# Four more turns behind each triangular solve's copies, a later due time for the last pair's transposes, and the decode queries' fill and rearrangement on other engines

## The chip, the cores and the metric

One NeuronCore of a Trainium2 chip runs the whole program in one launch. The metric is the device time of an execution in microseconds (us); the value for a kernel is the median of its runs.

## The reference

One inference step of a decoder layer: 512 prompt tokens of width 2048 and 8 decode tokens that attend to a cache. A norm, modulated by a conditioning vector (adaLN), is followed by one input projection w_in, whose columns feed two mixers: sliding-window attention (16 query heads, 4 key/value heads) and RWKV-7 (16 heads of 64 channels). Both outputs go through w_out; a SwiGLU FFN follows. Of mixer B this is what the change touches:

```python
def _wkv7_scan(S0, r, w, k, v, a, b):
    def step(S, inp):
        r_t, w_t, k_t, v_t, a_t, b_t = inp
        sa = jnp.einsum("bhij,bhj->bhi", S, a_t)
        S = S * w_t[:, :, None, :] + sa[..., None] * b_t[:, :, None, :] + v_t[..., None] * k_t[:, :, None, :]
        return S, jnp.einsum("bhij,bhj->bhi", S, r_t)
...
# mixer B, per head: y from the scan, then group norm over the 64 channels, bonus, gate
    y, S = _wkv7_scan(S0.astype(f32), r_h, hs(decay), k_h, v_h, -kk, kk * hs(a))
    mu = jnp.mean(y, axis=-1, keepdims=True)
    var = jnp.mean(jnp.square(y - mu), axis=-1, keepdims=True)
    y = ((y - mu) * lax.rsqrt(var + GN_EPS)).reshape(B, T, RWKV_WIDTH) * ln_w + ln_b
    bonus = jnp.sum(r_h * k_h * r_k.astype(f32), axis=-1, keepdims=True) * v_h
    y = (y + bonus.reshape(B, T, RWKV_WIDTH)) * g
...
# mixer A: sliding-window attention (window 128, ALiBi, sinks); w_out on both mixers' outputs; SwiGLU FFN
```

## The kernel before

All four engines and the DMA queues work on one stream. TensorE (PE) multiplies in three passes (a weight tile split into `wh` and `wl`, activations into `hH` and `hL`), two products of 260 columns each, so one k-step of a w_in or w_out tile is six matmuls. A weight tile is loaded by SP (`raw`), cast on ACT (`wh`) and subtracted on VectorE, DVE in the profile (`wl`), and serves four k-steps, 24 matmuls.

Stages: start (adaLN of this layer, norm), the RWKV part (140 to 920 us) with eight head pairs, attention with w_out beside it (from 915 us), then the FFN. In the RWKV part the w_in tiles (`main_tile`) are the filler, and everything else comes as generators ("jobs"). After each k-step `pump` adds 0.62 us to a planner's clock and resumes each job whose due time has passed; `self.done_at` is the due time that a job leaves behind, and wrapped engines add the estimated cost of what they issue. A bare `yield` hands the turn back until the next k-step. A scheduler then orders each engine's instructions by their dependences and this program order, so a shift of a job can move everything behind it.

The steps of one pair, in its order:

- prep: elementwise work on DVE, ACT and POOL, then products `pG` on PE, masked to `AB` on DVE, and rearranged through DRAM (`ABd`, tile `As`, queues of POOL and SP).
- solve (`rwkv_rest`): the inverse of 32x32 unit triangular blocks, 31 steps of two DVE operations on `Tt` (lines 721 and 724), with other DVE work between them. Its result goes to DRAM in four DMAs on POOL and SP (`TTd`, line 731), comes back in one on POOL (`Td`, line 732), and four DVE copies put it into the block-diagonal `TT`.
- turns: the loop of line 738 gives back the turn. Then two groups of four products `pu` = L3 x `TT` (shown as `pu<-TT,L`).
- chain: 16 steps on PE and ACT through `Z` (psum `psc`), the output products `pY`, the group norm on DVE and ACT (tile `RR`), line 804's due time, and four transposes of the normed `RR` (psum `pt2`, shown as `pt<-cst,RR`). Their result becomes `V`, is gated, written to DRAM (`catd`) and read back (`catl`) as input of w_out.

adaLN of the FFN runs beside the pairs in small products `ada<-ar,cT`, whose loads `ar` SP issues. SP's and POOL's queues are in order: an issue that waits holds all issues behind it.

Decode attention (`attn_decode`): the decode queries `QS` are rearranged by two DMAs into `QW` (lines 980 and 981), a tile `Q4` (in the profile `rstd`, whose buffer it takes) is zeroed (line 983), and eight DVE copies put `QS` and `QW` in it. Prompt attention issues logits `pl`, softmax on DVE (`Lg`, `sm`), transposes `pt<-cst,Lg` and the product `pO`, with w_out matmuls `po` as filler.

Of the kernel before, what the change touches and what calls it, by code (L numbers as in the profile page):

```python
# [63 lines left out]
class Kern:  # L64
# [642 lines left out]
    def rwkv_rest(self, d):  # L707
        nc, I, rc = self.px, self.I, self.rc
        hp, L3, PC = (d[n] for n in ("hp", "L3", "PC"))
# [25 lines left out]
        for c4 in range(4):  # L735
            ro = slice(32 * c4, 32 * c4 + 32)
            nc.vector.tensor_copy(TT[ro, :, 32 * c4:32 * c4 + 32], Td[ro])
        for _ in range(4):
            yield
        for e in range(2):  # L740
            pu = self.aux("pu")
# [59 lines left out]
        nc.scalar.activation(var, var, AF.Sqrt, bias=self.eps_g, scale=1.0 / 64)  # L801
        nc.vector.reciprocal(var, var)
        nc.vector.tensor_tensor(g3(yc), g3(yc), b3(var), ALU.mult)
        self.done_at = self.now() + 1.8
        yield
        pt = self.aux("pt2")
        for q in range(4):
# [164 lines left out]
    def attn_decode(self):  # L972
        nc, I, ap = self.px, self.I, self.ap
# [4 lines left out]
        QW = ap.tile([P, 8, 8], F32, name="QW")  # L978
        QS = self.QS.rearrange("p t h s -> p t (h s)")
        for b in range(2):  # L980
            nc.gpsimd.dma_start(QW[64 * b:64 * b + 64], QS[64 - 64 * b:128 - 64 * b])
        Q4 = xt("rstd")[:, 0:512].rearrange("p (a b c) -> p a b c", a=2, b=8)
        nc.gpsimd.memset(Q4, 0.0)
        yield
        for hg in range(2):
            rows = slice(64 * hg, 64 * hg + 64)
# [768 lines left out]
```

## Time and profile before

| | us |
|---|---|
| median of 3 runs | 2652.13 (2649.76 to 2660.87) |
| profiled execution | 2657.65 |
| its span in the profile | 2655.8 |
| PE busy | 2539.9 (96%) |
| DVE, ACT, POOL busy | 1648.6, 1166.6, 384.7 |
| granted TensorE clock, mean | 0.976 |
| PE idle, 140 to 920 us / 920 to 1050 us | 44.2 / 11.2 |

The span is the profiled execution from its first instruction to its last. A row of the timeline gives start, duration, engine, line, operation, out<-in, shapes, the count of like rows drawn together, and in brackets the engine's idle time before it with what released it. Line L49 is the wrapper through which the jobs issue, so most of the pairs' rows carry it and are told apart by their tiles.

### The profile page before, as it was taken

Reading aid. Unit: us, or ns where it says so; the run is one execution under the profiler, and the core shown is the slowest. Engines: PE = TensorE matmul, PEld = TensorE weight load, DVE = VectorE, ACT = ScalarE, POOL = GpSimd, SP = SyncE. Lnnn points to the kernel's source line nnn. Section 1 sums busy time; section 2 is a strip of 40 time slices with the busy share of each in tenths; the row PEclk is TensorE's granted clock in tenths of the full one; section 3 lists DMA queues with packets and bytes.
Section 4 is the critical chain, followed back from the end, with each engine's and each line's share of the span. In section 5 each row is a group of like instructions: output and inputs, shape, how many; then the busy total and the mean of one; then the engine's idle time right before and its main releaser. Section 6 shows DMA issues by size and latency. Waiting matters only on the chain. (4 is left out here: it accounts for less than half of the span.)

```text
span 2655.8 us, 58969 instructions
## 1 busy us (share of the span) xinstructions
PE 2539.9 (96%) x23373; PEld 2368.0 (89%) x23373; DVE 1648.6 (62%) x3627; ACT 1166.6 (44%) x2413; POOL 384.7 (14%) x532
## 2 busy tenths in 40 slices
PE   7898999899999999998999999999999999999998
PEld 4687878777788988898999999999999999999997
DVE  5465545465566454678877777777777763443456
ACT  3143556456555333457544444444444432222225
POOL 0011112121213110011121122122122000000003
PEclk9998999899999998999999999999999999999999
DMA  9865555455334574345586687687687452333333
GB/s 352 300 203 178 182 179 185 152 180 175 124 121 131 178 227 151 100 160 180 167 225 194 173 232 202 165 229 205 165 227 211 124 180 92 124 124 102 118 102 111
DMA packets 241701, 460.20 MB, mean 173 GB/s; under 512 B 32352, under 2 KB 44560, under 8 KB 241392
## 3 DMA queue, kind: packets, MB, share of 16 engines
q1 hardware_dynamic: 206160, 377.22, 43.1%
q0 software_dynamic: 34624, 78.16, 13.4%
q8 instruction: 183, 3.00, 0.5%
q10 hardware_dynamic: 640, 1.05, 0.2%
q14 instruction: 94, 0.77, 0.1%
HBM read 421.73 MB, written 35.59 MB: 172 GB/s over the span
## 5 line engine op out<-in xcount | busy, mean ns | idle before, releaser
L89 ACT CAST wh<-raw 128x512 fp32r<-128x512 f32 (+2 forms) x410 | 247.4, 606 | 490.4 <-PE pf L99 285.1
L92 DVE TENSOR_TENSOR wl<-raw,wh 128x512 fp32r<-128x512 f32 (+2 forms) x410 | 280.0, 686 | 246.8 <-ACT wh L89 230.8
L99 PE MATMUL pf<-go,wh 128*128 128x260 f32 x2560 | 414.1, 281 | 0.0
L99 PEld LDWEIGHTS pf<-go,wh 128*128 128x128 f32 x2560 | 354.0, 188 | 0.1
L1283 ACT CAST wh<-sr 128x512 fp32r<-128x512 f32 x320 | 198.0, 621 | 258.3 <-PE pm L1454 228.5
L99 PE MATMUL pm<-hH,wh 128*128 128x260 f32 (+1 forms) x1248 | 292.4, 312 | 7.6 <-ACT wh L89 6.8
L1284 DVE TENSOR_TENSOR wl<-sr,wh 128x512 fp32r<-128x512 f32 x320 | 220.3, 689 | 83.1 <-ACT wh L1283 76.0
L99 PE MATMUL pf<-go,wl 128*128 128x260 f32 x1280 | 267.7, 282 | 0.0
L99 PE MATMUL pm<-hH,wl 128*128 128x260 f32 (+1 forms) x1248 | 263.4, 290 | 4.2 <-DVE wl L92 4.2
L1454 PE MATMUL pm<-xT,wh 128*128 128x260 f32 x1408 | 263.2, 286 | 1.4 <-DVE pc L1531 1.1
L99 PE MATMUL pm<-hL,wh 128*128 128x260 f32 (+1 forms) x1248 | 260.4, 289 | 0.0
L1454 PE MATMUL pm<-T,wh 128*128 128x260 f32 x1408 | 257.7, 283 | 0.0
L99 PEld LDWEIGHTS pm<-hH,wh 128*128 128x128 f32 (+1 forms) x1248 | 195.9, 190 | 45.5 <-issue 18.7
L1454 PEld LDWEIGHTS pm<-xT,wh 128*128 128x128 f32 x1408 | 216.8, 188 | 7.9 <-DVE pc L1531 3.1
L1454 PEld LDWEIGHTS pm<-T,wh 128*128 128x128 f32 x1408 | 216.9, 188 | 0.0
L1454 PE MATMUL pm<-B0H,wl 128*128 128x260 f32 x704 | 200.8, 285 | 9.4 <-DVE wl L1284 9.0
L99 PEld LDWEIGHTS pm<-hH,wl 128*128 128x128 f32 (+1 forms) x1248 | 196.1, 190 | 13.8 <-DVE wl L92 7.1
L1454 PE MATMUL pm<-B0H,wh 128*128 128x260 f32 x704 | 200.4, 285 | 2.5 <-DVE acct L1220 1.7
L99 PEld LDWEIGHTS pf<-go,wl 128*128 128x128 f32 x1280 | 201.0, 188 | 0.0
L99 PEld LDWEIGHTS pm<-hL,wh 128*128 128x128 f32 (+1 forms) x1248 | 196.4, 191 | 4.7 <-issue 2.5
L1454 PE MATMUL pm<-T,wl 128*128 128x260 f32 x704 | 198.9, 282 | 0.1
L1454 PE MATMUL pm<-B0L,wh 128*128 128x260 f32 x704 | 198.9, 282 | 0.0
(426 smaller groups left out, 5266.8 us busy)
## 6 DMA issues: line engine op xcount, KB each, us to landing
ar<-in_w_ada SPq DMA_DIRECT2D x256, 256.0 KB, 4.0
sr<-in_w_fi SPq DMA_DIRECT2D x176, 256.0 KB, 4.3
raw<-in_w_fo SPq DMA_DIRECT2D x176, 256.0 KB, 2.7
raw<-in_w_in SPq DMA_DIRECT2D x144, 256.0 KB, 3.8
araw<-in_w_ada SPq DMA_DIRECT2D x64, 512.0 KB, 6.6
raw<-in_w_fi SPq DMA_DIRECT2D x120, 256.0 KB, 4.1
s<-in_w_fi SPq DMA_DIRECT2D x80, 256.0 KB, 5.5
s<-in_w_fi POOLq DMA_DIRECT2D x80, 256.0 KB, 7.2
```

Source lines behind the costliest of these rows:

```text
L89: nc.scalar.copy(wh[:, :n], raw[:, :n])
L92: nc.vector.tensor_tensor(wl[:, :n], raw[:, :n], wh[:, :n].bitcast(F32), ALU.subtract)
L99: nc.tensor.matmul(ps[:m, bank, :HB], w, a[:, k, h, :], start=first and i == 0, stop=last and i == 2, skip_group_check=True,)
L1283: nc.scalar.copy(H, src)
L1284: nc.vector.tensor_tensor(L, src, H.bitcast(F32), ALU.subtract)
L1454: nc.tensor.matmul(ps[:, :HB], x[:, s], y, start=g == k == i == 0, stop=g == 1 and k == 3 and i == 2, skip_group_check=True)
```

## The change

Three edits: eight bare yields for four between the copies into `TT` and the products `pu` (all pairs); for the last pair (hp 7) a due time 4.3 us instead of 1.8 behind the group norm; and in the decode part the two `QW` DMAs issued by SP instead of POOL, and the fill of `Q4` on DVE instead of POOL.

```diff
--- before.py
+++ after.py
@@ -735,7 +735,7 @@
         for c4 in range(4):
             ro = slice(32 * c4, 32 * c4 + 32)
             nc.vector.tensor_copy(TT[ro, :, 32 * c4:32 * c4 + 32], Td[ro])
-        for _ in range(4):
+        for _ in range(8):
             yield
         for e in range(2):
             pu = self.aux("pu")
@@ -801,7 +801,7 @@
         nc.scalar.activation(var, var, AF.Sqrt, bias=self.eps_g, scale=1.0 / 64)
         nc.vector.reciprocal(var, var)
         nc.vector.tensor_tensor(g3(yc), g3(yc), b3(var), ALU.mult)
-        self.done_at = self.now() + 1.8
+        self.done_at = self.now() + (1.8 if hp < 7 else 4.3)
         yield
         pt = self.aux("pt2")
         for q in range(4):
@@ -978,9 +978,9 @@
         QW = ap.tile([P, 8, 8], F32, name="QW")
         QS = self.QS.rearrange("p t h s -> p t (h s)")
         for b in range(2):
-            nc.gpsimd.dma_start(QW[64 * b:64 * b + 64], QS[64 - 64 * b:128 - 64 * b])
+            nc.sync.dma_start(QW[64 * b:64 * b + 64], QS[64 - 64 * b:128 - 64 * b])
         Q4 = xt("rstd")[:, 0:512].rearrange("p (a b c) -> p a b c", a=2, b=8)
-        nc.gpsimd.memset(Q4, 0.0)
+        nc.vector.memset(Q4, 0.0)
         yield
         for hg in range(2):
             rows = slice(64 * hg, 64 * hg + 64)
```

What it does to the order of instructions in the RWKV part. The table counts, for each pair, what PE has between the pair's last `pG` and its first `pu`, and how many DVE instructions that are not the solve's stand between its first step and its last, before -> after:

| pair | w_in matmuls | ada products | other DVE instructions in the solve |
|---|---|---|---|
| 1 | 181 -> 186 | 96 -> 85 | 15 -> 15 |
| 2 | 203 -> 197 | 96 -> 80 | 20 -> 17 |
| 3 | 191 -> 204 | 96 -> 103 | 15 -> 15 |
| 4 | 227 -> 174 | 80 -> 80 | 25 -> 6 |
| 5 | 179 -> 186 | 80 -> 96 | 15 -> 8 |
| 6 | 175 -> 184 | 112 -> 80 | 11 -> 10 |
| 7 | 187 -> 250 | 80 -> 64 | 9 -> 8 |
| 8 | 227 -> 230 | 0 -> 0 | 20 -> 28 |

Pair 4's solve on DVE shows it closest. Its last steps before (`stmp` and `Tt` are the solve; `tF`, `KB` are the next pair's preparation, `wl` and `lf` weight tiles):

```order
L724 TENSOR_TENSOR Tt<-Tt,stmp_5922 128x7x4
L49 SCALAR_TENSOR_TENSOR tA_5840<-tF_5740,tA_5840 128x512
L721 TENSOR_TENSOR stmp_5931<-Tt,As 128x24
L92 TENSOR_TENSOR wl_6275<-raw_6272,wh_6274 128x512
L724 TENSOR_TENSOR Tt<-Tt,stmp_5931 128x8x3
L49 TENSOR_TENSOR tF_5740<-tF_5740,tD_5842 128x512
L721 TENSOR_TENSOR stmp_5934<-Tt,As 128x16
L92 TENSOR_TENSOR lf_6332<-raw_6333,lf_6332 128x256
L724 TENSOR_TENSOR Tt<-Tt,stmp_5934 128x8x2
L49 TENSOR_TENSOR KB_6294<-tF_5740,tC_5996 128x16x32
L721 TENSOR_TENSOR stmp_5953<-Tt,As 128x8
L724 TENSOR_TENSOR Tt<-Tt,stmp_5953 128x8
```

And its last steps in the changed kernel:

```order
L721 TENSOR_TENSOR stmp_5966<-Tt,As 128x28
L724 TENSOR_TENSOR Tt<-Tt,stmp_5966 128x7x4
L721 TENSOR_TENSOR stmp_5975<-Tt,As 128x24
L724 TENSOR_TENSOR Tt<-Tt,stmp_5975 128x8x3
L721 TENSOR_TENSOR stmp_5978<-Tt,As 128x16
L724 TENSOR_TENSOR Tt<-Tt,stmp_5978 128x8x2
L721 TENSOR_TENSOR stmp_5997<-Tt,As 128x8
L724 TENSOR_TENSOR Tt<-Tt,stmp_5997 128x8
L49 TENSOR_SCALAR tA_6048<-tA_6048 128x512
```

The next pair's elementwise work no longer stands between the steps.

The last pair's transposes on PE (`pt_...<-cst,RR`; `pm` are w_in tiles, the numbers name the weight tiles) before:

```order
L99 MATMUL pm_11122<-hL,wh_11169 128x260 x2
L99 MATMUL pm_11122<-hH,wl_11170 128x260 x2
L99 MATMUL pm_11122<-hH,wh_11169 128x260 x2
L99 MATMUL pm_11122<-hL,wh_11169 128x260 x2
L99 MATMUL pm_11122<-hH,wl_11170 128x260 x2
L99 MATMUL pm_11122<-hH,wh_11199 128x260
L49 MATMUL pt_1552_11141<-cst,RR_9622 128x128 x4
L99 MATMUL pm_11122<-hH,wh_11199 128x260
L99 MATMUL pm_11122<-hL,wh_11199 128x260 x2
```

and in the changed kernel:

```order
L99 MATMUL pm_11252<-hH,wh_11285 128x260 x2
L99 MATMUL pm_11252<-hL,wh_11285 128x260 x2
L99 MATMUL pm_11252<-hH,wl_11286 128x260 x2
L99 MATMUL pm_11252<-hH,wh_11285 128x260 x2
L99 MATMUL pm_11252<-hL,wh_11285 128x260 x2
L99 MATMUL pm_11252<-hH,wl_11286 128x260
L49 MATMUL pt_1571_11301<-cst,RR_9655 128x128 x4
L99 MATMUL pm_11252<-hH,wl_11286 128x260
L99 MATMUL pm_11252<-hH,wh_11285 128x260 x2
```

Before they stand behind the first matmul of a new weight tile, now behind the seventeenth of the 24 that a tile serves. From the last pair's `pY` to them there were 67 w_in matmuls and are 59; 335 w_in matmuls followed them and 247 follow now.

The first logits of prompt attention on PE (`po_12103` and the next `po` are two output tiles of w_out, 12136 and 12188 weight tiles) before:

```order
L99 MATMUL po_12103<-cH_11273,wh_12136 128x260 x2
L99 MATMUL po_12103<-cL_11274,wh_12136 128x260 x2
L99 MATMUL po_12103<-cH_11273,wl_12137 128x260 x2
L99 MATMUL po_12103<-cH_11273,wh_12136 128x260 x2
L99 MATMUL po_12103<-cL_11274,wh_12136 128x260 x2
L99 MATMUL po_12103<-cH_11273,wl_12137 128x260 x2
L49 MATMUL pl_12158<-Kt,q_12081 128x128
L49 MATMUL pl_12159<-Ks,q_12081 128x128
L49 MATMUL pl_12158<-Kt,q_12081 128x256
```

and in the changed kernel:

```order
L99 MATMUL po_12185<-cH_11398,wh_12188 128x260 x2
L99 MATMUL po_12185<-cL_11399,wh_12188 128x260 x2
L99 MATMUL po_12185<-cH_11398,wl_12189 128x260 x2
L99 MATMUL po_12185<-cH_11398,wh_12188 128x260 x2
L99 MATMUL po_12185<-cL_11399,wh_12188 128x260 x2
L99 MATMUL po_12185<-cH_11398,wl_12189 128x260 x2
L49 MATMUL pl_12212<-Kt,q_12081 128x128
L49 MATMUL pl_12213<-Ks,q_12081 128x128
L49 MATMUL pl_12212<-Kt,q_12081 128x256
```

The logits stood in the last weight tile of `po_12103`; now a further 24 w_out matmuls stand ahead of them. On SP the two `QW` transfers now stand between two loads of w_out tiles, and the fill stands on DVE between two `wl`.

## The prediction

> **What bounds the kernel now.** I read the busy table first, then the waits of TensorE in the two stretches that the change reaches, then the single waits in time order.
>
> ```profile
> PE 2539.9 (96%) x23373; PEld 2368.0 (89%) x23373; DVE 1648.6 (62%) x3627; ACT 1166.6 (44%) x2413; POOL 384.7 (14%) x532
> PEclk9998999899999998999999999999999999999999
> ```
>
> PE is the bound: 116 us of the 2655.8 us span are idle, so only a PE wait, or time at a lower clock, can be won. The next two views are PE's waits from 140 to 920 us (the eight head pairs of the recurrent part) and from 920 to 1050 us (start of attention): what waited <- for what, us in total, times, longest.
>
> ```profile
> PE pu L49 <- DVE TT L49: 17.2, 6, 5.0
> PE psc L49 <- ACT Z L49: 8.8, 13, 1.8
> PE pt L49 <- DVE RR L49: 5.6, 1, 5.6
> ...
> PE pt L49 <- DVE sm L49: 5.9, 1, 5.9
> PE pl L49 <- issue: 4.9, 1, 4.9
> 140.00:920.00 780.00, 735.80 (x8416) 637.71 (x8415) 453.30 (x1105) 400.04 (x987) 144.21 (x197) 0.95 0.51 164
> ```
>
> The last row is a window (start:end, length, busy PE, PEld, DVE, ACT, POOL, then granted clock, DMA share, GB/s): 44.2 us of PE idle in the first stretch, and a clock of 0.95. The 17.2 us stand exactly where edit one puts its turns. PE's rows there, in time order (start, duration, operation, idle before it and its releaser):
>
> ```profile
> 250.27 0.65 PE L322 MATMUL ada<-ar,cT 128*32 128x128 f32 x8 [5.67 <-DMA ar<-in_w_ada]
> 254.46 0.77 PE L49 MATMUL pu<-TT,L 128*128 128x128 f32 x2 [3.02 <-DVE TT L49]
> 328.74 0.38 PE L49 MATMUL pu<-TT,L 128*128 128x128 f32 x1 [1.21 <-DVE TT L49]
> 388.74 0.47 PE L49 MATMUL pu<-TT,L 128*128 128x128 f32 x1 [2.93 <-DVE TT L49]
> 491.86 0.58 PE L49 MATMUL pu<-TT,L 128*128 128x128 f32 x1 [5.05 <-DVE TT L49]
> 562.87 0.58 PE L49 MATMUL pu<-TT,L 128*128 128x128 f32 x1 [1.82 <-DVE TT L49]
> 711.41 0.46 PE L49 MATMUL pu<-TT,L 128*128 128x128 f32 x2 [3.19 <-DVE TT L49]
> ```
>
> These are pairs 1 to 5 and 7; pairs 6 and 8 do not wait. What ends last is the chain behind the solve, here pair 4's on VectorE:
>
> ```profile
> 479.64 0.18 DVE L724 TENSOR_TENSOR Tt<-Tt,stmp 128x8 f32<-128x8 f32 x1
> 490.62 1.18 DVE L49 COPY TT<-Td 32x256 f32<-32x256 f32 x4 [6.52 <-DMA Td<-TTd]
> DMA to landing us min/median/max: 4.0/5.0/6.3
> ```
>
> From the last solve step to the last copy it is 12 us, most of it two DMAs, one behind the other (the last row is the second's time from issue to landing, line 732, over the eight pairs). No edit shortens this chain; more PE work can only be put beside it.
>
> **Edit one, eight turns for four.** One turn is a k-step of six w_in matmuls. Their spacing is:
>
> ```profile
> 951.69 0.40 PE L99 MATMUL po<-cH,wl 128*128 128x260 f32 x2
> 951.93 0.40 PE L99 MATMUL po<-cH,wh 128*128 128x260 f32 x2
> ```
>
> 0.12 us each, so a turn is 0.73 us and four turns 2.9 us, if all four are spent behind the copies. They are not: the order is chosen again, and the table in the section on the change gives the net effect. Per pair, with 0.12 us a w_in matmul and some 0.06 us a small ada product (eight in 0.65 us above):
>
> - Pair 1 gets 5 more w_in matmuls and 11 fewer ada products ahead of pu: nothing. Its 3.02 and 5.67 us are one wait, on the solve: SP issues two of the TTd copies, the loads of `ar` are queued behind them, and an ada product that needs one stands right at pu. I keep 8.7 us.
> - Pair 2: 6 w_in and 16 ada fewer, -1.7 us of cover, against 1.9 us less other VectorE work inside the solve (estimated from the order's shapes). About 1 us of the 1.21 stays.
> - Pair 3: 13 w_in more, 1.6 us, and a few small products. Of 2.93 us some 0.6 stay.
> - Pair 4: 53 w_in fewer, -6.4 us; but the reciprocals and elementwise work between the solve steps go (the first piece of order below the diff), an estimated 11 us. Line 721's steps here span 29.7 us, pair 7's 21.6 (instructions of one line in pair 4's and in pair 7's window; the count, ns min/median/max, first and last start):
>
> ```profile
> L721 DVE TENSOR_TENSOR stmp<-Tt,As x31: 133/249/1222, 449.7 to 479.4; 128x60 f32<-128x60 f32 x3, 128x28 f32<-128x28 f32 x2, 128x54 f32<-128x54 f32 x2, 128x48 f32<-128x48 f32 x2
> ...
> L721 DVE TENSOR_TENSOR stmp<-Tt,As x31: 168/251/1008, 679.7 to 701.3; 128x60 f32<-128x60 f32 x3, 128x28 f32<-128x28 f32 x2, 128x54 f32<-128x54 f32 x2, 128x48 f32<-128x48 f32 x2
> ```
>
>   At pair 7's speed the solve is 8 us shorter, more than the 6.4 lost: of 5.05 us some 0.5 to 3.5 stay, I take 1.
> - Pair 5: 7 w_in and 16 ada more, 1.8 us: gone. Pair 7: 63 w_in more, 7.6 us against 3.19: gone.
>
> Together 1.21+2.93+5.05+1.82+3.19 = 14.2 us, less 2.6 that stay: **-11.6 us**, with bounds of 0 (the waits only move) and -14.2.
>
> Behind the waits the clock was low (windows as above, the clock third from last):
>
> ```profile
> 388.70:392.10 3.40, 3.36 (x15) 2.67 (x15) 0.00 (x0) 1.09 (x2) 0.00 (x0) 0.52 0.20 74
> 491.70:495.10 3.40, 3.24 (x56) 3.02 (x57) 0.80 (x2) 0.59 (x1) 0.20 (x1) 0.50 0.15 39
> 562.70:566.10 3.40, 3.23 (x15) 3.23 (x16) 3.33 (x6) 0.88 (x2) 1.36 (x1) 0.53 0.16 51
> 711.40:714.80 3.40, 3.39 (x24) 2.83 (x25) 0.69 (x1) 1.86 (x4) 0.00 (x0) 1.00 0.00 0
> ```
>
> Three of four 3.4 us windows behind a wait ran at about 0.5, each losing 1.7 us: 5 us if all return. But 3.19 us of wait at 711 cost no clock and 1.82 at 562 did, so the length of the wait alone does not decide, and small products around the same places may keep it low (rival 5). I take **-3.5 us** (bounds 0 and -5.1).
>
> **Edit two, 4.3 for 1.8 in the last pair.**
>
> ```profile
> 876.66 0.69 PE L49 MATMUL pt<-cst,RR 128*128 128x128 f32 x2 [5.56 <-DVE RR L49]
> ```
>
> A later due time would put matmuls ahead of the transposes. The second piece of order shows none: they have moved by eight w_in matmuls within the tiles, to an earlier place if anything: 59 w_in matmuls behind the last pY instead of 67, with the same group norm on VectorE between. **0 us**, bounds -5.6 (wait gone) and +1.0 (8 matmuls less cover). What the wait of 5.56 us costs in clock stays too.
>
> **Edit three, fill and rearrangement off POOL's queue.** The two transfers and the fill themselves, and what waited for them:
>
> ```profile
> 921.46 1.06 POOL L49 DMA_DIRECT2D QW<-QS  x2 [0.38 <-issue]
> 922.51 0.55 POOL L49 MEMSET rstd<- 128x512 f32 x1
> 923.09 0.25 DVE L49 COPY rstd<-QS 64x16 f32<-64x16 f32 x2 [2.22 <-POOL rstd L49]
> ...
> DMA to landing us min/median/max: 5.5/5.6/5.7
> ```
>
> PE's only wait from 920 to 960 us:
>
> ```profile
> PE po L99 <- ACT wh L89: 0.4, 1, 0.4
> ```
>
> So the 2.22 us of VectorE's wait and the 0.55 us of fill, now on VectorE, are worth nothing directly. On SP the two issues (1.06 us on POOL) now stand ahead of loads of w_out; PE's 0.4 us there was all that reached it from such a tile; uncovered the issues cost 1 us. The Trainium skill ("DMA: Bandwidth & Descriptors", Latency and other measured facts) gives about 1 us to the first byte from POOL's queue and 0.6 from SP's: 0.4 us of a 5.6 us transfer, hidden as well.
>
> What it does change is the order after it. PE's two long waits of this stretch:
>
> ```profile
> 948.90 16.14 SPq L49 DMA_DIRECT2D q<-qd  x4
> 960.60 0.55 PE L49 MATMUL pl<-Kt,q 64*128 64x128 f32 x1 [4.91 <-issue]
> DMA to landing us min/median/max: 11.6/12.3/12.9
> ...
> 1013.97 0.62 ACT L144 CAST cH<-catl 128x512 fp32r<-128x512 f32 x1 [6.29 <-DMA catl<-catd]
> 1016.23 0.47 PE L49 MATMUL pt<-cst,Lg 128*128 128x128 f32 x1 [5.89 <-DVE sm L49]
> 1013.50:1020.30 6.80, 4.07 (x16) 3.02 (x17) 3.40 (x14) 1.61 (x3) 0.00 (x0) 0.50 0.48 157
> ```
>
> The first logits waited 4.91 us for the load of `q`, issued at 948.90 and landed some 11.6 us later. In the third piece of order they stand 24 matmuls later, 2.9 us: **-2.9** (bounds 0 and -4.9). At 1016 PE waited for softmax work on VectorE, which stood behind the cast of `catl` on ACT, which waited 6.29 us for its load. In the new order some 78 w_out matmuls (9.4 us) stand between the first pO and the next attention product, and the cast overlaps them: **-4** (bounds 0 and -5.9). The 6.8 us at 0.50 around it lose 3.4 us; I take **-2** (bounds 0 and -3.4).
>
> **The sum.** A new order of 1766 rows on PE will make small waits of its own; the old order has 13 on `Z` of 8.8 us in all, so I allow **+3** (bounds -4 and +9). -11.6 -3.5 +0 -2.9 -4 -2 +3 = **-21 us**. The profiled execution took 2657.65 us (span 2655.8), so 2636.7; the median of the runs, 2652.13, lies 5.5 us under that execution, so I forecast **2631 us**.
>
> **Rivals.**
>
> 1. *The waits only move* (0.26). Where pu no longer waits for TT, PE meets the next late thing: `Z` in the chain behind pu (13 waits already), or the later pt2. For it: the chain solve-to-TT is unchanged, and pair 4's cover shrinks by 6.4 us. Against it: pairs 6 and 8 show that a pair can pass without a wait. Then edit one gives -2, the rest -5: 2645 us; with edit three also empty, 2652.
> 2. *Slower: loads queue behind the solve* (0.08). SP's queue is in order, and its TTd copies wait for the solve:
>
> ```profile
> 243.30 1.33 SPq L731 DMA_DIRECT2D TTd<-Tt  x2
> 245.38 1.81 SPq L317 DMA_DIRECT2D ar<-in_w_ada  x4
> ```
>
>    In pair 1 the `ar` loads behind them cost 5.67 us of PE. More turns ahead of pu use up loaded tiles sooner. If in all seven other pairs an ada product stands ahead of pu whose load is queued behind TTd, each pays 5.7 in place of the 14.2 in all: 7 x 5.7 - 14.2 = +26, less 9 from edit three: 2669 us. It decides from the point where such a load's use is less than about 6 us behind the solve's end. Against it: in the new order only pairs 3 and 5 have one such load ahead of pu, 2 to 3 us before it, which is 9 us behind the solve's end.
> 3. *Edit two does what it says* (0.07): 5.56 us and 1.7 to 3.4 of clock more, 2623 us.
> 4. *Decode costs PE* (0.05): the fill on VectorE (0.55 us) and `QW` on SP delay `wl` and a load; 2 to 4 us at each of two places, and no gain from edit three: 2645 us.
>
> 5. *The clock stays low* (0.12). At 711 a wait of 3.19 us cost no clock and one of 1.82 us at 562 was followed by 3.4 us at 0.53, and the ada products and the pairs' 32- and 64-row products lie around the same places; then the low windows do not come from these waits and stay. The sum loses its terms of 3.5 and 2: 2636.5 us. The Trainium skill ("TensorE: Matmul & The Clock Gate", What's actually happening) has the clock halve after at least one idle window of about 3.4 us, counted on a free-running grid; by that rule the waits of 1.8 to 3.2 us would not do it alone, which is this rival; the windows at 388 and 562, directly behind such waits, speak for the forecast.
>
> **How the numbers follow.** The forecast has 0.42. A measurement of this kernel tells about 0.5% from no change: 13.3 us, so below 2639 or above 2665. Faster by more: most of the forecast (0.38), rival 3 (0.07), most of rival 5 (0.09) and the good end of rival 1 (0.06): 0.60. Slower: most of rival 2, 0.07. The rest is within: 0.33. The range takes the forecast's bounds as far as they are likely to fall together (-38 us: 2614) and, above, rival 1 with its empty end and a little over (2656): **2614 to 2656**.
>
> **What would show it.** Right: PE's waits on TT fall from 17.2 to about 5 us, with pair 1's pair of waits kept; pair 4's solve takes some 21 us; pt waits for RR still 5 to 6 us in the last pair; pl and pt at the start of attention wait 2 us each. Wrong: PE's waits on `ar` or `Z` grow by as much as those on TT fall; the clock of the 140 to 920 stretch stays 0.95; the wait on RR gone.

## The result and the profile after

| | median, us | runs | ratio to before, 95% interval |
|---|---|---|---|
| before | 2651.39 (2648.54 to 2660.87) | 6 | |
| changed | 2633.22 (2630.48 to 2636.15) | 6 | 0.9928 [0.9912, 0.9945] |

The change makes the kernel 18 us faster; 2631 was forecast. The total came out, but not by the terms of the sum. The profiled execution of the changed kernel has a span of 2630.3 us, 25.5 less than the one of before. The medians here and below are those of the fast executions; the one slow execution, 11271 us in e3, is in none of them.

The first two lines of the changed kernel's page:

```profile
PE 2526.8 (96%) x23373; PEld 2359.7 (90%) x23373; DVE 1650.7 (63%) x3628; ACT 1167.3 (44%) x2413; POOL 382.3 (15%) x529
PEclk9998999999999997999999999999999999999999
```

PE's instructions are the same in number, and its busy time fell by 13.1 us: the same matmuls ran faster. Windows over two stages of before and then of the changed kernel show where. The first reaches from 140 us to the first w_out matmul, the second from there to the first FFN product:

```profile
140.00:919.50 779.50, 735.30 (x8412) 637.21 (x8411) 453.30 (x1105) 399.54 (x986) 144.17 (x196) 0.95 0.51 164
919.50:1211.30 291.80, 272.91 (x2301) 250.64 (x2300) 168.45 (x541) 128.55 (x322) 38.47 (x66) 0.95 0.51 161
...
140.00:892.70 752.70, 717.87 (x8461) 627.04 (x8455) 458.12 (x1115) 401.21 (x990) 142.30 (x196) 0.97 0.53 170
892.70:1189.20 296.50, 279.55 (x2301) 254.74 (x2300) 168.72 (x543) 128.98 (x322) 38.00 (x63) 0.94 0.52 160
```

The recurrent part is 26.8 us shorter, the w_out part 4.7 us longer. In the first, PE's idle time (length less busy time) fell from 44.2 to 34.8 us, and the clock rose from 0.95 to 0.97. The trace's clock records give that more closely: the stretches at half clock add up to 71.6 us before and 41.0 after, so with half of each lost, 35.8 and 20.5 us. (PE is idle for 8.2 and 6.2 us of these stretches, and idle time loses nothing by a lower clock; without it the loss is 31.8 and 17.4 us. All figures below count the whole stretches.) Waits gave 9.4 us, the clock 15.3 by this count. The FFN, which the change does not reach, differs by about 3 us between the two profiles.

PE's waits in the recurrent part of the changed kernel, and the single waits for TT and for the last pair's RR:

```profile
PE pu L49 <- DVE TT L49: 18.4, 5, 10.1
PE psc L49 <- ACT Z L49: 6.7, 12, 1.9
PE pt L49 <- DVE RR L49: 4.8, 4, 1.7
...
259.17 0.55 PE L49 MATMUL pu<-TT,L 128*128 128x128 f32 x1 [10.05 <-DVE TT L49]
336.63 0.60 PE L49 MATMUL pu<-TT,L 128*128 128x128 f32 x3 [3.03 <-DVE TT L49]
484.13 0.35 PE L49 MATMUL pu<-TT,L 128*128 128x128 f32 x1 [0.78 <-DVE TT L49]
623.86 0.35 PE L49 MATMUL pu<-TT,L 128*128 128x128 f32 x1 [3.58 <-DVE TT L49]
788.11 0.38 PE L49 MATMUL pu<-TT,L 128*128 128x128 f32 x1 [0.91 <-DVE TT L49]
862.03 0.44 PE L49 MATMUL pt<-cst,RR 128*128 128x128 f32 x2 [1.65 <-DVE RR L49]
```

The sum on TT looks unchanged (17.2, now 18.4), and read alone it would say that the edit failed. But pair 1's two waits, 5.67 on `ar` and 3.02 on TT, are now one of 10.05 on TT. Without pair 1 the waits on TT went from 14.2 us to 8.3, and the wait on `ar` is gone from the list. Pairs 3, 5 and 7 no longer wait; pairs 6 and 8, which did not, now do.

### The profile page after: what moved, and what is told of

Its sections match the earlier page's. It is cut to its first block, busy times and chain, and to the rows that moved or that the text cites. A ratio compares the mean times of both kernels' runs of the same rounds, so it can differ in the third digit from the quotient of the medians.

```text
span 2630.3 us, 58954 instructions
## 1 busy us (share of the span) xinstructions
PE 2526.8 (96%) x23373; PEld 2359.7 (90%) x23373; DVE 1650.7 (63%) x3628; ACT 1167.3 (44%) x2413; POOL 382.3 (15%) x529
```

## The experiments

In every table and text below, "w_in part" is the first window above, its half-clock loss is worked out in the same way, and ratios are to runs of the kernel before on the same chip. A profile is one execution of its kernel and not always a typical one: that of e4 is the slowest of its twelve, 9 us above their median, that of e6 lies 8 us above its median and that of e9 8 us below.

**The edits one by one, and more turns.** e1 holds edit one alone, e2 edit two, e3 edit three; e4 is the changed kernel with twelve turns.

```diff
 e1
-        for _ in range(4):
+        for _ in range(8):
 e2
-        self.done_at = self.now() + 1.8
+        self.done_at = self.now() + (1.8 if hp < 7 else 4.3)
 e3
-            nc.gpsimd.dma_start(QW[64 * b:64 * b + 64], QS[64 - 64 * b:128 - 64 * b])
+            nc.sync.dma_start(QW[64 * b:64 * b + 64], QS[64 - 64 * b:128 - 64 * b])
...
-        nc.gpsimd.memset(Q4, 0.0)
+        nc.vector.memset(Q4, 0.0)
 e4 (against the changed kernel)
-        for _ in range(8):
+        for _ in range(12):
```

> Edit one alone (eight turns for four). Theory 1, from the trace of the changed kernel: the whole gain is in the part up to 920 us and is this edit's, 9 us of PE waits and 15 us of half clock; the ratio to before is 0.988 to 0.993, the end of w_in comes 22 to 28 us earlier, and the last pair's wait for RR is near 1.7 us without edit two. Theory 2, the sizes of the prediction: -12 of waits, -3.5 of clock, a ratio of 0.994 to 0.9955, the wait for RR stays 5 to 6 us.

> Edit two alone (due time 4.3 us in the last pair). In the order of instructions only a few rows of PE, VectorE and ACT change places, and the transposes stay where they were. Theory 1: ratio 0.999 to 1.001, wait for RR 5 to 6 us. Rival: the due time itself ends the wait for RR (1.7 us in the changed kernel), ratio 0.997 to 0.998.

> Edit three alone (QW's transfers on SP, the fill on VectorE). Theory 1, from the trace of the changed kernel: the stretch from the first w_out matmul to the first of the FFN takes 296 us instead of 292, mostly by half clock behind the decode products; ratio 1.000 to 1.003. Theory 2, the prediction: the waits before pl and pt shrink by 9 us together, ratio 0.996 to 0.997.

> The changed kernel with twelve turns instead of eight. If the waits for TT that are left (3.0, 0.8, 3.6 and 0.9 us behind pairs 2, 4, 6 and 8) are a matter of cover, four more turns (2.9 us) end most of them: 3 to 6 us, ratio 0.989 to 0.991. If the gain of eight turns came from where the small products fall among the w_in matmuls, there is no trend: ratio anywhere from 0.988 to 1.000, and the time goes with the sum of half-clock stretches up to the end of w_in (20 us in the changed kernel, 36 before), not with the waits.

| | median, us | ratio, 95% interval |
|---|---|---|
| before | 2656.17 | |
| e1, eight turns alone | 2627.66 | 0.9892 [0.9869, 0.9915] |
| e2, due time alone | 2657.22 | 1.0012 [0.9995, 1.0028] |
| e3, decode alone | 2659.06 | 1.0015 [0.9996, 1.0033] |
| e4, twelve turns | 2645.78 | 0.9955 [0.9934, 0.9975] |

The whole gain is edit one's; neither of the others shows a gain. The last pair's transposes in e2 and e1 decide who ended the wait for RR:

```profile
874.11 0.48 PE L49 MATMUL pt<-cst,RR 128*128 128x128 f32 x1 [5.66 <-DVE RR L49]
...
864.68 0.33 PE L49 MATMUL pt<-cst,RR 128*128 128x128 f32 x1 [1.66 <-DVE RR L49]
```

With the due time alone (first row) the wait stands at 5.66 us; with the turns alone (second row) it is 1.66, as in the changed kernel. How the turns did it is read on VectorE: before and in the changed kernel, the last output products `pY` and the reduction that begins the group norm:

```profile
858.76 1.23 DVE L49 TENSOR_TENSOR stt<-sS,X 128x1024 f32<-128x1024 f32 x1 [5.48 <-DMA sS<-in_st]
861.67 1.17 PE L49 MATMUL pY<-Z,RR 128*32 128x64 f32 x64
869.20 0.68 DVE L49 TENSOR_REDUCE L<-pY 128x8 f32<-128x512 f32 x1
...
851.91 1.17 PE L49 MATMUL pY<-Z,RR 128*32 128x64 f32 x64
855.36 0.68 DVE L49 TENSOR_REDUCE L<-pY 128x8 f32<-128x512 f32 x1
```

Before, the decode state's work (`stt`, `sS`) had waited 5.48 us for a load, stood ahead of the group norm, and the reduction came 7.5 us behind the start of `pY`. Now it comes 3.5 us behind. The same work still stands ahead of it and still waits for its load, 3.70 us, but it starts 7.0 us ahead of `pY` (at 844.91) instead of 2.9.

In e3 the waits for `pl` and `pt` are gone as forecast, and another has come:

```profile
PE plx L49 <- DVE sm L49: 5.5, 1, 5.5
```

The w_out part takes 295.1 us there, against 291.8 and 292.8 in before and e2. PE's idle time in it did fall, to 14.5 us from 18.9 before, but half clock loses 20.3 us of it against 15.4. Where the 5.5 us come from, the changed kernel's timeline shows across four engines:

```profile
926.47 13.64 SPq L49 DMA_DIRECT2D q<-qd  x4
940.21 7.91 SPq L87 DMA_DIRECT2D raw<-in_w_out  x4
946.41 1.23 ACT L89 CAST wh<-raw 128x512 fp32r<-128x512 f32 x2 [11.93 <-DMA raw<-in_w_out]
947.06 0.69 DVE L92 TENSOR_TENSOR wl<-raw,wh 128x512 fp32r<-128x512 f32 x1 [8.60 <-ACT wh L89]
947.67 0.48 DVE L49 CUSTOM_DVE_ANT_0 Lg<-pl,bias,der 128x256 f32<-128x256 f32 x1
948.62 0.21 PE L49 MATMUL plx<-KVS,rstd 64*32 64x1 f32 x1 [5.52 <-DVE sm L49]
```

Four issues of `q` loads hold SP from 926.47 to 940.11, since the last one's buffer is not free; behind them stands a w_out tile's load; the cast waits for it, `wl` for the cast, the softmax work for `wl`, and PE for the softmax. The logits now stand behind that tile's `wl` on VectorE.

e4 speaks against a trend. Its first pair gains what twelve turns promise: PE's waits there (on `ar` and on TT, up to 270 us) are

```profile
PE ada L322 <- DMA ar<-in_w_ada: 3.7, 1, 3.7
PE pu L49 <- DVE TT L49: 1.6, 1, 1.6
```

5.3 us in place of 10.1. But behind it the waits on TT are 15.6 us where eight turns alone have 10.2, and the half-clock loss of the w_in part is 37.5 us against 22.2. The granted clock of all executions, not only of the profiled one, points the same way: 0.9761 on average in e4, 0.9815 in e1, 0.9754 in the kernel before.

**Six turns, and three tries at a better place.** e5 has six turns and nothing else; e6 and e7 are e1 with small products given in smaller portions; e8 is e1 with twelve turns for the first pair.

```diff
 e5 (against before)
-        for _ in range(4):
+        for _ in range(6):
 e6 (against e1), in the loop over c of the pA products
+            if hp < 2 and c in (5, 10):
+                yield
 e7 (against e1), at the end of the decode value products
-            yield
+                yield
 e8 (against e1)
-        for _ in range(8):
+        for _ in range(12 if hp == 0 else 8):
```

> The kernel before with six turns for four, nothing else changed. If the turns work as cover (2 x 0.73 us more beside each chain), the waits for TT behind pairs 2 to 8 lie between those of four turns (14 us) and eight turns (10 us), and the ratio between 0.993 and 0.997. If the gain comes from where the order happens to fall, six turns show no such place between: waits or half clock up to the end of w_in can lie outside those of four and eight turns, ratio anywhere from 0.985 to 1.000, and the length of the w_in part follows the sum of its PE idle time and its half-clock loss.

> Eight turns alone, and in the first two pairs the 32 pA products given in three parts, with a turn (six w_in matmuls) between. Theory: a 3.4 us stretch filled by small products, without any idle time, sets the clock to half in the next one. Then the two half-clock stretches behind these products (near 208 and 287 us, 6.8 us each, 3.4 us lost each) end, and w_in 1200 comes 4 to 7 us earlier than with eight turns alone, less what pair 1 and 2 lose in cover (2 to 3 us each). Rival, idle time alone lowers the clock: both stretches stay, and w_in 1200 comes no earlier.

> Eight turns alone, and the decode part's value products given in eight parts of 9 instead of four of 18, with a turn between. Theory of small products: half clock from the start of w_out to the FFN loses under 10 us instead of 16.5, and this stretch takes 286 to 289 us instead of 293; ratio 0.986 to 0.988 if eight turns alone are 0.989. Rival: the other jobs due in the same turns fill the place with small products of their own, and the loss stays above 14 us.

> Eight turns, twelve for the first pair. The first pair's PE wait (9.4 us with eight turns, 8.7 with four, 1.6 in the kernel with twelve turns everywhere) is 1 to 3 us, with the half clock around it (5.1 us) down to 0 to 3.4. If the pairs behind it keep what eight turns gave, the ratio is 0.983 to 0.987. If the order behind it falls apart as with twelve turns everywhere, it is 0.990 to 0.996 in spite of the first pair's gain.

| | median, us | ratio, 95% interval |
|---|---|---|
| before | 2652.85 | |
| e5, six turns | 2656.86 | 1.0019 [0.9998, 1.0041] |
| e6, pA split | 2639.67 | 0.9944 [0.9926, 0.9962] |
| e7, decode values split | 2633.87 | 0.9931 [0.9910, 0.9952] |
| e8, twelve for the first | 2637.80 | 0.9947 [0.9928, 0.9966] |

Six turns cover as expected: behind pairs 2 to 8 the waits on TT are 11.4 us, between 14.2 (four) and 10.2 (eight). And the kernel is no faster. So cover alone is not what eight turns gained: PE's idle time in the w_in part is 38.6 us (44.2 before, 35.2 in e1), but its half-clock loss is 30.7 us, as with four turns, and the part takes 775.6 us. Idle time and half clock are together 11 us less than before, the part is 4 us shorter; the rest is open.

e6 met its two places differently. Two windows of 3.4 us behind and within pair 1's pA products, first of e1 and then of e6:

```profile
209.61:213.02 3.41, 3.41 (x57) 3.13 (x59) 0.69 (x1) 0.00 (x0) 0.29 (x1) 1.00 0.62 156
213.02:216.43 3.41, 3.41 (x37) 3.02 (x37) 0.69 (x1) 0.45 (x1) 1.04 (x2) 0.50 0.56 153
...
207.61:211.03 3.42, 3.42 (x74) 2.90 (x73) 0.00 (x0) 0.00 (x0) 0.87 (x1) 1.00 0.87 204
211.03:214.44 3.41, 3.41 (x42) 3.23 (x43) 1.81 (x3) 0.62 (x1) 0.73 (x2) 1.00 0.66 225
```

There the half clock ended, with no idle time in either kernel. At pair 2 it did not: a window with 6 w_in matmuls and 32 pA products was still followed by 10 us at half clock, and the lost cover cost more (5.6 us of wait at pair 2's pu, 3.3 in e1); w_in matmul 1200 came 1.3 us earlier than in e1, not 4 to 7. What made e6 slower than e1 came behind these two pairs: its w_in part is 766.8 us (e1 755.3), with 40.4 us of idle time (35.2), 29.0 of half-clock loss (22.2) and 16.6 of waits on TT behind pairs 2 to 8 (10.2). e7 gained nothing: half clock in the w_out part lost 25.6 us; transposes and logits of the other jobs fell into the same turns, as its rival has it. e10 below, without the split, shows 24.9, so how far the split itself did harm stays open. e8 gained on the first two pairs (w_in matmul 1200 came 11.8 us earlier than in e1) and lost it behind them, where the waits on TT were 11.6 us (10.2 in e1); its w_in part is 756.8 us, e1's 755.3. The 1.4 us more on TT are a small part of the 13 us that it lost there; the rest is open.

**The changed kernel and eight turns again, and a buffer of its own for `kst`.** The tile of the new key rows, `kst`, takes one of the four buffers of `q`, so the fourth `q` load waits for its store. e9 is the changed kernel and e10 is e1 once more; e11 and e12 are these two with

```diff
-        kt = ap.tile([8, 256], F32, tag="q", bufs=4, name="kst")
+        kt = ap.tile([8, 256], F32, tag="kst", bufs=1, name="kst")
```

> The changed kernel itself again, beside the three others of this job on one chip. It gave 0.9928 [0.9912, 0.9945] on its chip, eight turns alone 0.9892 [0.9869, 0.9915] on another. If edit three costs 2 to 4 us (1.0015 alone), it lies 0.001 to 0.002 above e10; if the two first figures differ by chip or by chance, both agree within 0.001. Half clock up to the end of w_in within 8 us of the 20.5 of its first profile.

> Eight turns alone again, on the same chip as e9: 0.989 to 0.993. With edit two's 1.0012 and edit three's 1.0015 taken as real costs, 0.001 to 0.003 below e9.

> The changed kernel with a buffer of its own for the new key rows (kst) instead of one of the four of q. PE's order is the same; on SP the fourth q load no longer waits for kst's store, and the q loads stand earlier, with no load of w_out behind a waiting one. Theory: edit three gave its gain back there (PE's plx wait of 5.5 us, for softmax work on VectorE behind a wl, whose load stood on SP behind the q loads). Then this wait falls below 2 us, the stretch from w_out to the FFN takes 285 to 292 us instead of 296, and the ratio is 0.002 to 0.004 below e9. Rival: the wait passes to the next load or product there, and the stretch stays at 294 to 297 us.

> Eight turns alone with the buffer of its own for kst. The wait of pl for q (3.2 us) goes, the one of pt behind catl's load (5.9 us) stays: w_out to FFN 287 to 291 us instead of 293, ratio 0.001 to 0.002 below e10. It beats e11 if edit three costs by itself, and loses to it if edit three's removal of the pt wait is worth its 4 us once the q loads are out of the way.

| | median, us | ratio, 95% interval |
|---|---|---|
| before | 2659.75 | |
| e9, the changed kernel | 2634.49 | 0.9911 [0.9889, 0.9934] |
| e10, eight turns alone | 2628.21 | 0.9889 [0.9866, 0.9911] |
| e11, changed, own kst | 2626.52 | 0.9887 [0.9864, 0.9910] |
| e12, eight turns, own kst | 2620.15 | 0.9862 [0.9839, 0.9884] |

The wait that edit three had made, in e9 and in e11:

```profile
PE plx L49 <- DVE sm L49: 4.9, 1, 4.9
...
PE plx L49 <- DVE sm L49: 1.2, 1, 1.2
```

The wait falls as the theory says, with PE's order unchanged, and the w_out part takes 294.0 us against 299.5 (292 at most was expected). In e12 `pl` no longer waits, `pt` still waits 6.3 us behind `catl`'s load, and the w_out part takes 285.7 us (287 at least was expected). This part varies by itself: the same kernel shows 292.9 us in e1 and 301.9 in e10, 296.5 in the changed kernel and 299.5 in e9, so a few us of it in one profile prove nothing; the wait's place does. e12 is the fastest version seen, about 14 us below the changed kernel on the same chip; it carries neither edit two nor edit three. Edit three cost 1.0015 alone, and with edit two 0.0022 between e9 and e10 and 0.0025 between e11 and e12. Each difference is within its intervals; all have one sign.

The buffer gained 0.0027 without edits two and three (e10 to e12) and 0.0024 with them (e9 to e11). So the wait on `plx` is not shown to be what edit three lost: with that wait nearly gone, e11 stays as far behind e12 as e9 is behind e10. The w_out parts of e11 and then e12:

```profile
892.40:1186.40 294.00, 278.94 (x2301) 253.62 (x2300) 169.12 (x545) 128.82 (x323) 38.10 (x63) 0.94 0.53 161
891.50:1177.20 285.70, 269.59 (x2301) 248.07 (x2300) 169.16 (x542) 128.92 (x322) 38.27 (x66) 0.96 0.53 166
```

PE's idle time is about the same, 15.1 and 16.1 us, and the clock differs: half clock loses 17.1 us in e11 and 11.9 in e12. In e3 too the loss stood in the clock. But this loss is 16.5 us in e1 and 24.9 in e10, one kernel, so that edit three lowers the clock is a reading of these profiles and not shown.

## Why the prediction was right, and where it was not

The time came to about 2 us of the forecast (2633 for 2631, faster). That is luck in part, since the steps came out otherwise: of the prediction's own signs, pair 4's shorter solve was seen (19.4 us for some 21), but the last pair's wait for RR, which was to stay at 5 to 6 us, fell to 1.65, and its end was named as a sign of being wrong. By its steps:

- **Edit one, waits on TT: -11.6 forecast, -5.9 measured** (14.2 to 8.3 without pair 1, in these two profiles; the means of three profiles with four turns and of seven with eight are 16.8 and 8.3, a gain of 8.5). Pairs 5 and 7 went to nothing as said, and so did pair 3. Pair 4's argument held: its solve, 29.7 us before, now spans

```profile
L721 DVE TENSOR_TENSOR stmp<-Tt,As x31: 168/253/1078, 454.6 to 474.0; 128x60 f32<-128x60 f32 x3, 128x28 f32<-128x28 f32 x2, 128x54 f32<-128x54 f32 x2, 128x48 f32<-128x48 f32 x2
```

  19.4 us, 10 less against some 11 estimated, and 0.78 us of its wait stay. Pair 2 kept 3.03 us where 1 was taken, and pair 6 waits 3.58 where none was expected: the step treated a pair without a wait as safe and priced only the pairs that waited. The price of a small ada product, 0.06 us, came from eight that ran at half clock; at full clock 32 of them take 1.08 us, 0.034 each, which is a small error. Pair 1 kept its wait, 10.05 us for 8.7. No product waits for `ar` there any more, but PE's work ahead of pu still ends 1 us behind the solve's last step (at 249.1 and 248.0 us), so PE waits for nearly the whole chain to TT.
- **Idle time in all: -11.6 and +3 of new waits, -8.6 forecast, -9.4 measured.** The parts changed places. Beside TT's 5.9 us, the waits on `ar` outside pair 1 (2.3), 2.1 us on `Z` and 2.0 of `adT` on RR went; pair 1 took 1.4 more; the last pair's wait for RR lost 3.9 us, three earlier pairs' transposes together gained 3.1, and small new waits make up the rest.
- **Clock: -3.5 forecast, -15.3 measured in the two profiles.** This is the term that was mis-sized. Low stretches at 388, 491 and 562 us, behind waits on TT, went as hoped, and the one at 491 was 6.8 us long where one window of 3.4 was counted: 6.8 us of loss in place of 5.1, of which 3.5 were taken. Not counted were the stretch behind the last pair's wait for RR (873 us, 3.4 lost), one with ada products and 1.65 us of idle time ahead of it (620 us, 3.4), and one behind pA products with no idle time at all (515 us, 3.4). All of them went, and one came (625 us, 1.7, behind pair 6's new wait). Over all profiles the gain is less: the half-clock losses of that part are 35.8, 27.3 and 30.7 us with four turns (before, e2, e3; mean 31.3), and 17.1 to 22.2 in seven profiles with eight turns (mean 20.0; e6 and e8, whose order differs in the RWKV part, show 29.0 and 22.2). So some 11 us of clock and 13 of idle time (45.9 to 33.3, means of the same profiles), of a part that is 28 us shorter. The 4 us that remain are not explained; the part's length less both differs by as much between two profiles of the changed kernel (697.4 and 693.7 us). The granted clocks of all executions agree in sign: over the whole kernel the loss (span times one less the clock) is 6 to 17 us less in e1 and e9 to e12 than in the kernel before on the same chip.
- **Edit two: 0 forecast; 1.0012 [0.9995, 1.0028] measured.** The order showed it. But the last pair's wait, forecast to stay because "the same group norm" lay between, fell by 3.9 us with edit one. The step that failed took the chain for one of fixed length, though a load's wait on VectorE stood in it.
- **Edit three: -8.9 forecast, 1.0015 [0.9996, 1.0033] measured, +3 to +5 us of the w_out part in the profiles.** Both waits named, for `q` and behind `catl`, did go, and the 24 matmuls did cover the first. The waits moved: 5.5 us on `plx` behind the held loads, and a half-clock loss of 18.8 us in this part against 15.4. So the step failed in two places: it counted both waits as won without asking what would wait next, and took -2 us for the clock where +3.4 came (+4.9 in e3). Rival 1, waits that only move, was right here and wrong for edit one. The range's bounds for this term (0 at worst) did not allow a loss.

The total was right by luck, because two errors cancelled: the clock of the recurrent part gave some 8 to 12 us more than taken, edit three 12 to 14 less. The forecast's sign and size rested on edit one, and e1 shows that alone to be 0.9892 [0.9869, 0.9915].

Settled: edit one makes the gain; edit two does not end the wait for RR; edit three's wait on `plx` comes from loads held on SP, since e11 takes it away. Open: what edit three lost, since taking that wait away did not bring its gain back. Read from traces but not shown by an experiment: how much of the clock's gain is due to the waits that went (10.2 us of the 17 lost at those places lay behind waits on TT and RR) and how much to small products that now fall elsewhere. e5 shows that more cover alone does not bring it, e4 that more turns need not bring more cover, and e6 ended one of two such places. Not tried: spreading the small products without shifting the rest of the order.

## What to carry to other kernels

A change of a few turns in such a planner is a new order for everything behind it: four, six, eight and twelve turns gave ratios of 1, 1.002, 0.989 and (with the other two edits) 0.9955, with no trend to read off. Add up PE's idle time and its half-clock time by stage before and after, since the list of waits shows only the first; and when a wait is to be covered, look also at the pairs that do not wait yet, and at what the in-order queues hold behind the load that is moved. Judge a stage by several executions, since one kernel's profiles differ by as much as the terms of such a sum.

## What the runs showed of the hardware that was not expected

The clock drops without any idle time. PE's rows ahead of the low stretch at 208 us, in the kernel before, and two windows there:

```profile
204.91 2.05 PE L49 MATMUL pA<-tC,KB 64*64 64x32 f32 x32
206.89 0.41 PE L322 MATMUL ada<-ar,cT 128*32 128x128 f32 x2
207.23 3.07 PE L49 MATMUL pA<-tC,KB 64*64 64x32 f32 x32
...
204.53:207.94 3.41, 3.41 (x50) 3.03 (x49) 1.14 (x4) 0.00 (x0) 1.11 (x1) 1.00 0.84 214
207.94:211.35 3.41, 3.41 (x47) 3.26 (x48) 0.69 (x1) 0.00 (x0) 0.17 (x1) 0.50 0.16 54
```

PE is busy for all of the first window, 44 of its 50 matmuls are products of 64 rows and 32 columns, and the second runs at 0.50. All changes of the clock in a profile lie on one grid of 3.41 us: every stretch between two changes is a whole multiple of it. That bears on a question that the prediction left, a wait of 3.19 us that cost no clock beside one of 1.82 that did:

```profile
559.47:562.88 3.41, 1.59 (x15) 1.16 (x13) 1.17 (x5) 1.07 (x4) 0.00 (x0) 1.00 0.07 21
...
706.23:709.65 3.42, 1.99 (x17) 1.78 (x15) 0.37 (x1) 0.62 (x1) 1.48 (x6) 1.00 0.42 134
709.65:713.06 3.41, 1.65 (x15) 1.68 (x16) 1.14 (x4) 0.48 (x1) 0.00 (x0) 1.00 0.00 0
```

The wait of 1.82 us lies in one window of the grid (idle 3.41 - 1.59) and the window behind it ran at 0.50. The wait of 3.19 us is split over two, 1.4 and 1.8 us, and neither was followed by a lower clock. So the place of a wait on the grid may count, but these windows do not show that it decides: the 1.76 us of idle time in the last one are almost as much as the 1.82, and a window with 1.65 us (617.5 to 620.9) was followed by half clock too. What PE does in the rest of a window differs as well: 15 products of 128x128 in the last one, 8 w_in matmuls and four narrow `psc` products in the one at 559, 9 w_in matmuls and 12 ada products in the one at 617. The grid lies elsewhere in each execution. One kernel in two executions, e1 and e10, has low stretches that begin at 213.03 and 208.70 us, not a whole number of steps apart; it lost 22.2 and 17.1 us to half clock in the w_in part and 16.5 and 24.9 in the w_out part, and these differences are more than most of the single terms of the sum.
